# The first token block's second FFN product done plainly in two passes, with the other block's Strassen weight sums made in the second pass

## The chip, the cores and the metric

The kernel runs on one core of one Trainium2 chip. The metric is the time of one execution on the device, in microseconds (us); lower is better. PE is TensorE, DVE is VectorE, ACT is ScalarE, POOL is GpSimd, SP is SyncE, whose queue issues most of the DMAs here.

## The reference, cut to what matters

One layer of a streaming encoder: 16 meta tokens and 2048 tokens of width 1024 go through an S5 mixer with a gated linear unit, and then through a gated ConvFFN. The change lies in the ConvFFN alone, in its last product:

```python
def conv_ffn(xn, w_up, conv_w, conv_b, w_down):
    h = causal_dwconv(xn @ w_up, conv_w, conv_b)
    a, b = jnp.split(h, 2, axis=-1)
    return (jax.nn.silu(a) * b) @ w_down
```

Here `w_up` is 1024 x 5632, the convolution has 3 taps, and `w_down` is 2816 x 1024 (22 row blocks of 128). The result is added to the stream. The last 2048 rows are the output.

## The kernel before, in words

**Precision.** Each float32 operand is split into two float16 parts, high and low. A product is three matmuls (`mm3`, lines 75 to 78): high by high, high by low, low by high. All matmuls here are 128x128 by 128x512.

**Blocks.** The FFN runs twice, for kb = 0 and kb = 1, on 1024 tokens each. For each block `up` (line 1134 on) multiplies by `w_up` with 7 Strassen products per pair of column blocks, 22 pairs `m` in all, and `conv` does the convolution, the gate and the split of the activation into `act16[:, f, r, hi/lo, 512 tokens]`, where f is one of the 22 row blocks of `w_down` (NF = 22, NH = 11) and r is the half of the tokens. Then `down(kb)` multiplies by `w_down`.

**Strassen in `down`.** Both matrices are seen as 2 x 2: the activation by token half r and by f below or above 11, the weight by row half and by column half (512 columns). Seven products replace eight, in four stages with 2, 2, 2 and 1 products (`STAGES`). Each product takes 11 steps j, and each step is 4 token tiles (t4) of 3 matmuls, so `down` has 7 x 11 x 12 = 924 matmuls. The operands of a product are sums: the activation sums are made by `mix` (lines 1206 to 1220: POOL, DVE, ACT, DVE), 44 of them per block, with two scratch tiles that lie in the free part of `hc`; `add11` in `conv` (line 1119, POOL) makes one more sum for the rows above 11.

**Weights.** Every weight tile `wc` (128 x 2 x 512 float16, high and low) is a "unit". The units of both blocks stand in one list in the order of their use, and each takes the next of NR = 9 slots in turn. `w_unit` makes a unit for kb = 0: it has rows of `w_down` in one of NW = 4 staging tiles `fst` (float32, 512 KB, loaded by `w_load` on SP's queue); for 5 of 7 products POOL adds or subtracts two parts of it in place (lines 874 and 879); ACT writes the high part (line 880). `w_flush` then writes the low part on DVE (line 886), stores the unit to the DRAM buffer `wcd` from SP (line 887), and issues the next staging load if this unit was the last that uses its tile (lines 829 to 834). For kb = 1 a unit is only reloaded from `wcd` (line 859). `w_units(n + LD)` runs 5 units ahead of the matmuls. A flush happens only at the next call.

**Other traffic in `down(0)`.** `turn_hd` (line 1336) transposes the second block's inputs from DRAM into `hc` by DMA, 7 pairs, six of them in stage 0 at every second step. `load_res` brings the residual stream to tiles `res`, DVE adds the product to it (line 1323), and ACT's queue stores it to the output.

**Order.** The order on each engine is the order in which the program is written out; nothing reorders it. `later(d, fn)` puts a piece of work d ticks on, and `tick` is called once per `up` product and per `down` product step.

Of the kernel before, what the change touches and what calls it, by code (L numbers as in the profile page):

```python
# [15 lines left out]
P = 128  # L16
# [28 lines left out]
def tile_kernel(ctx: ExitStack, tc: tile.TileContext, x, meta, norm_mix, norm_ffn, w_in, lam_re, lam_im, log_dt,  # L45
# [20 lines left out]
    wcd = dram.tile([231, P, 2, 512], F16, name="wcd")  # L66
# [730 lines left out]
    kept = {u[:1] + u[2:]: i for i, u in enumerate(u for u in units if u[1] == 0)}  # L797
    for u in units:
        if u[1]:
            continue  # L800
        if u[0] == "u":
            need = [u[:3] + (0,)] + [u[:3] + (1,)] * (u[3] not in (1, 2))
        else:
            need = [u[:4] + (0,)] + [u[:3] + (u[3] // 2 * 2, 1)] * (u[2] == 2)
        for l in need:
            users[l] = u
            if l not in loads:
                loads.append(l)
    wst, wc, wtmp, ring, w_los, tdone = {}, {}, {}, {}, [], set()
# [6 lines left out]
    def w_load():  # L816
        if pos["load"] < len(loads):
            l = loads[pos["load"]]
            t = wst[l] = fw.tile([P, D], F32, tag="wst", bufs=NW, name=f"fst{pos['load']}")
            if l[0] == "u":  # L820
                m, ab = divmod(l[2], 2)
                c = 2 * m + NF * ab + l[3]
                SY.dma_start(out=t.rearrange("p (dk n) -> p dk n", n=P),
                             in_=w_up[0].rearrange("(dk p) n -> p dk n", p=P)[:, :, c * P:(c + 1) * P])
            else:
                s, j, i = l[2:]
                wd = w_down[0].rearrange("(a j p) (b n) -> j p a b n", a=2, p=P, n=512)[j]
                if s == 3:
                    SY.dma_start(out=t, in_=w_down[0, j * P:(j + 1) * P])
                elif i == 0:  # L830
                    SY.dma_start(out=t.rearrange("p (a n) -> p a n", a=2), in_=wd[:, :, int(s == 0)])
                else:
                    k = min(2, NH - j)
                    SY.dma_start(out=t.rearrange("p (a n) -> p a n", a=2)[:, 0:k],
                                 in_=w_down[0].rearrange("(f p) n -> p f n", p=P)[:, NH + j:NH + j + k, 512:1024])
            pos["load"] += 1
# [13 lines left out]
    def w_unit():  # L850
# [7 lines left out]
        if units[n][1]:  # L858
            SY.dma_start(out=w, in_=wcd[kept[units[n][:1] + units[n][2:]]])
            return  # L860
        if units[n][0] == "u":
# [5 lines left out]
            src = wtmp.pop((x_, m)) if i == 5 else st[src[0]][:, src[1]]  # L867
        else:
            k, kb, s, j, i = units[n]
            t = wst[k, kb, s, j, 0]  # L870

            if s == 2:
                src = t[:, hi_ if i == 0 else lo_]
                PO.tensor_tensor(src, src, wst[k, kb, s, j // 2 * 2, 1][:, hi_ if j % 2 else lo_], op=ALU.add)
            elif i == 1:
                src = t[:, hi_ if s == 0 else lo_]
            else:
                src, oth = (t[:, lo_], t[:, hi_]) if s in (0, 3) else (t[:, hi_], t[:, lo_])
                PO.tensor_tensor(src, src, oth, op=ALU.add if s == 3 else ALU.subtract)
# [3 lines left out]
    def w_flush():  # L883
        while w_los:
            w, src, u = w_los.pop(0)
            V.scalar_tensor_tensor(w[:, 1], src, GS, w[:, 0], op0=ALU.mult, op1=ALU.subtract)  # L886
            SY.dma_start(out=wcd[kept[u[:1] + u[2:]]], in_=w)
            for l in [l for l in wst if users[l] == u]:
                del wst[l]
                w_load()  # L890
# [198 lines left out]
    def conv(kb, m, e):  # L1089
# [12 lines left out]
        def taps():  # L1102
            V.scalar_tensor_tensor(y, hu[:, 1:17], cwt[:, 1, c:c + 1], y, op0=ALU.mult, op1=ALU.add)  # L1103
            V.scalar_tensor_tensor(y, hu[:, 0:16], cwt[:, 0, c:c + 1], y, op0=ALU.mult, op1=ALU.add)
            if ab and f < NH:
                for r, dst in ((0, yr[:, 0]), (1, actr[:, f, 1])):
                    V.scalar_tensor_tensor(dst, actr[:, f, r], AS, yr[:, r], op0=ALU.mult, op1=ALU.mult)
            elif ab:
                V.scalar_tensor_tensor(y, act[:, f], AS, y, op0=ALU.mult, op1=ALU.mult)

# [11 lines left out]
        if ab == 0:  # L1122
            later(6, lambda: A.activation(y, y, AF.Silu))
        elif f < NH:
# [104 lines left out]
    CTAG = {"12": (fl, "hu1"), "21": (fl, "hu1"), "11": (fl, "hu0"), "22": (fp, "yb")}  # L1229

    def down(kb):
# [8 lines left out]
        def load_res(c, q):  # L1240
            tt, cs_ = part(c, q)
            pool, tag = CTAG[c]
# [4 lines left out]
        def store_res(c, q, t):  # L1247
            tt, cs_ = part(c, q)
            for e in range(2):
                A.dma_start(out=o4[e, rows, tt, cs_][:, t], in_=res[c, q][64 * e:64 * e + 64, t])  # L1250

# [28 lines left out]
        if kb == 0:  # L1280
            for i, b in enumerate((0, 4, 8, 20, 12, 16)):
                put(0, 2 * i, turn_hd, b, b + 4)
            put(3, 1, turn_hd, 24, 28)

        for s, prods in enumerate(STAGES):
# [32 lines left out]
            for t4, i in banks:  # L1318
                for j in range(NH - 2, NH):
                    down_mm(j, t4, i)  # L1320
                for c, sign in prods[i][1:]:
                    h = res[c, t4 // 2][:, t4 % 2]
                    V.scalar_tensor_tensor(h, po[t4, i], sign / (GS * AS), h, op0=ALU.mult, op1=ALU.add)  # L1323
# [49 lines left out]
```

## Time and profile before

| what | value |
|---|---|
| runs | 2129.42, 2134.12, 2137.76 us; median 2134.12 us |
| the profiled execution | 2128.21 us; its span 2126.4 us, 1.8 us less |
| mean granted PE clock | 0.962 |
| `up(0)` | 770.6 to 1205.4 us |
| `down(0)` | 1205.4 to 1519.6 us |
| `up(1)` | 1519.6 to 1918.6 us |
| `down(1)` | 1918.6 to 2126.4 us |

The four stretches are cut where the first matmul of each begins. A matmul's own duration in the profile (380 ns) is longer than its share of PE's time, because matmuls overlap in the pipeline; the pace is read by counting matmuls in a window in which PE never stops. "Idle before" is time in which an engine did nothing before instructions of a group, with the instruction that released it. A DMA share of 1.00 means that all 16 DMA engines were busy all the time.

### The profile page before, as it was taken

What the parts mean: (1) busy time and instruction counts of PE and PEld (TensorE: products, weight loads), DVE (VectorE), ACT (ScalarE), POOL (GpSimd) and SP (SyncE); (2) the same over time, 40 slices, a digit from 0 to 9 for tenths busy, and PEclk for the clock granted to TensorE, in tenths of its full rate; (3) what the DMA queues carried; (4) which work ended last, traced back from release to release, by engine and by line L of the source; (5) the groups of instructions that cost most, each with busy time, mean ns of one, the idle gap of its engine ahead of it and who ended that gap; (6) DMA issues with size and microseconds to landing.
All of it is one profiled execution on the core that took longest, in us unless ns stands there. A gap on an engine that the chain in (4) does not pass through costs nothing. (4 is left out here: it accounts for less than half of the span.)

```text
span 2126.4 us, 29078 instructions
## 1 busy us (share of the span) xinstructions
PE 1925.9 (91%) x10860; PEld 954.7 (45%) x10860; DVE 1518.7 (71%) x2084; ACT 644.8 (30%) x1083; POOL 689.3 (32%) x727
## 2 busy tenths in 40 slices
PE   4688999699999999999999867676999999999999
PEld 3456556455444444444444323232444444444444
DVE  4489988944443459999999987954466666668882
ACT  4432322312222234444344422212122223232110
POOL 5221211410000025554666774734100001116740
PEclk9998999799999999999999989888999999999999
DMA  9956666957665565444434659554733333336443
GB/s 203 196 116 132 146 127 150 224 155 171 132 157 134 137 166 181 158 147 152 149 127 151 170 156 267 156 168 150 232 104 101 103 100 104 101 103 159 133 121 98
DMA packets 333449, 315.50 MB, mean 148 GB/s; under 512 B 149740, under 2 KB 237372, under 8 KB 333308
## 3 DMA queue, kind: packets, MB, share of 16 engines
q1 hardware_dynamic: 315388, 271.59, 49.4%
q0 software_dynamic: 8496, 27.30, 4.7%
q10 hardware_dynamic: 9424, 14.76, 2.6%
q8 instruction: 85, 1.39, 0.3%
q14 instruction: 56, 0.46, 0.1%
HBM read 175.17 MB, written 102.69 MB: 131 GB/s over the span
## 5 line engine op out<-in xcount | busy, mean ns | idle before, releaser
L78 PE MATMUL p<-hc,wc 128*128 128x512 f16 x1232 | 468.8, 381 | 6.5 <-DVE wc L886 6.5
L76 PE MATMUL p<-hc,wc 128*128 128x512 f16 x1232 | 468.8, 381 | 1.9 <-DMA hc<-hl 1.9
L77 PE MATMUL p<-hc,wc 128*128 128x512 f16 x1232 | 468.6, 380 | 0.9 <-DMA hc<-hl 0.9
L137 PE MATMUL g<-wg,yT 128*128 128x512 f16 x1536 | 334.2, 380 | 0.8 <-DMA yT<-yh 0.8
L77 PE MATMUL po<-wc,act 128*128 128x512 f16 x616 | 244.7, 397 | 80.4 <-DVE wc L886 80.4
L76 PE MATMUL po<-wc,act 128*128 128x512 f16 x616 | 243.5, 395 | 8.5 <-DVE res L1323 3.7
L78 PE MATMUL po<-wc,act 128*128 128x512 f16 x616 | 244.4, 397 | 0.0
L137 PEld LDWEIGHTS <-yT 128*128 128x128 f16 x1536 | 150.5, 98 | 182.9 <-issue 2.6
L886 DVE SCALAR_TENSOR_TENSOR wc<-fst,wc 128x512 f16<-128x512 f32 x209 | 199.0, 966 | 44.4 <-ACT wc L880 34.5
L880 ACT ACTIVATE wc<-fst 128x512 f16<-128x512 f32 x209 | 125.6, 625 | 245.0 <-POOL fst L847 120.3
L78 PEld LDWEIGHTS <-wc 128*128 128x128 f16 x1232 | 120.8, 98 | 154.7 <-DVE wc L886 8.8
L77 PEld LDWEIGHTS <-wc 128*128 128x128 f16 x1232 | 120.7, 98 | 139.9 <-issue 1.9
L76 PEld LDWEIGHTS <-wc 128*128 128x128 f16 x1232 | 120.6, 98 | 140.1 <-issue 3.5
L76 PE MATMUL u<-hnT,win 128*128 128x512 f16 (+2 forms) x352 | 113.1, 331 | 26.9 <-DMA hnT<-hl 17.0
L78 PEld LDWEIGHTS <-act 128*128 128x128 f16 x616 | 62.3, 101 | 163.5 <-issue 98.4
L1218 DVE TENSOR_TENSOR hc<-hc,hc 128x512 f32<-128x512 f32 x66 | 86.5, 1323 | 68.7 <-POOL hc L1216 42.7
L1219 ACT CAST act<-hc 128x512 f16<-128x512 f32 x88 | 54.2, 618 | 244.9 <-DVE hc L1218 148.0
L77 PE MATMUL u<-hnT,win 128*128 128x512 f16 (+2 forms) x352 | 112.9, 331 | 9.9 <-DMA hnT<-hl 9.9
L78 PE MATMUL u<-hnT,win 128*128 128x512 f16 (+2 forms) x352 | 112.7, 330 | 0.0
L1095 ACT ACTIVATE act<-hu,cwt 128x1024 f32<-128x1024 f32 x44 | 54.6, 1241 | 178.5 <-DVE hu L1187 129.8
L1095 ACT ACTIVATE y<-hu,cwt 128x1024 f32<-128x1024 f32 x44 | 54.6, 1241 | 162.3 <-DVE hu L1187 122.8
L1216 POOL TENSOR_TENSOR hc<-act 128x512 f32<-128x512 f16 x66 | 90.5, 1378 | 37.7 <-DVE hc L1218 37.7
(366 smaller groups left out, 3024.7 us busy)
## 6 DMA issues: line engine op xcount, KB each, us to landing
wcd<-wc SPq DMA_DIRECT2D x231, 256.0 KB, 2.3
wc<-wcd SPq DMA_DIRECT2D x231, 256.0 KB, 2.6
fst<-in_ffn_w_down_dram SPq DMA_DIRECT2D x49, 512.0 KB, 4.7
fst<-in_ffn_w_up_dram SPq DMA_DIRECT2D x44, 512.0 KB, 5.0
ud<-us SPq DMA_DIRECT2D x32, 258.0 KB, 4.8
U<-ud SPq DMA_DIRECT2D x16, 516.0 KB, 6.9
Toep<-kd SPq DMA_DIRECT2D x64, 128.0 KB, 5.5
yd<-yf POOLq DMA_DIRECT2D x8, 1024.0 KB, 6.5
```

What stands on the lines that cost most here:

```text
L76: PE.matmul(out=ps, lhsT=sh, rhs=mh, start=first, stop=False)
L77: PE.matmul(out=ps, lhsT=sh, rhs=ml, start=False, stop=False)
L78: PE.matmul(out=ps, lhsT=sl, rhs=mh, start=False, stop=last)
L137: PE.matmul(out=gps[t][o], lhsT=yT[t][:, a, dk], rhs=wg[b][:, dk, 512 * o:512 * o + 512], start=(dk == 0 and a + b == 0), stop=(dk == DK - ...
L880: A.activation(w[:, 0], src, AF.Copy, scale=GS)
L886: V.scalar_tensor_tensor(w[:, 1], src, GS, w[:, 0], op0=ALU.mult, op1=ALU.subtract)
L1095: A.activation(y, hu[:, 2:18], AF.Identity, bias=cwt[:, 3, c:c + 1], scale=cwt[:, 2, c:c + 1])
L1216: PO.tensor_tensor(t_, act16[:, fa_, ra, 1], act16[:, fb, rb, 1], op=op)
L1218: V.tensor_tensor(s_, s_, t_, op=ALU.add)
L1219: A.copy(act16[:, fd, rd, 0], s_)
```

## The change

For kb = 0 `down` no longer uses Strassen. It makes two passes, r = 0 and r = 1, over all 22 row blocks f; each step has both column halves n = 1, 0 and four token tiles, so a step is 24 matmuls, a pass 528, and both 1056. Eight PSUM banks hold a pass.

The units of kb = 0 are now: in pass 0 the 44 plain tiles ("p", row block f, column half n), made from a staging tile without any sum; in pass 1 the same 44 tiles, reloaded from `wcd`, and between them the 55 sums ("x", five for each j of 11) that kb = 1 needs, made by POOL, ACT and DVE and stored to `wcd`, but used by no matmul of kb = 0. The two Strassen tiles of kb = 1 that are no sums are plain tiles (`key`). Pass 1 loads all 22 row blocks of `w_down` into staging again, two for each j. Two of the five sums of a j are written to no staging half and share one buffer (`wtmp`). So `wcd` has 253 entries, and the first block's `mix` and `add11` are gone; `hi_all` and `lo_all` split a whole row block at once, for f below 11 too, where only half of it was split before. The seven pairs of transposes stand in pass 0 at f = 2, 4, .. 14, the residual loads of each pass at f = 6 and 8. In the last two steps of pass 1 the lead of the units is 2 instead of 5. `up`, and `down(1)` with its 924 matmuls and 77 reloads, stay as they were.

```diff
     for kb_ in range(2):
...
-        units += [("d", kb_, s, j, i) for s, n in ((0, 2), (1, 2), (2, 2), (3, 1)) for j in range(NH) for i in range(n)]
+        if kb_ == 0:
+            sums = [("x", 0, s, j, i) for j in range(NH) for s, i in ((1, 0), (2, 0), (0, 0), (2, 1), (3, 0))]
+            for r in range(2):
+                for f in range(NF):
+                    units += [("p", 0, r, f, 1), ("p", 0, r, f, 0)]
+                    units += sums[len(sums) * f // NF:len(sums) * (f + 1) // NF] if r else []
+        else:
+            units += [("d", 1, s, j, i) for s, n in ((0, 2), (1, 2), (2, 2), (3, 1)) for j in range(NH) for i in range(n)]
+    def key(u):
+        if u[0] == "u":
+            return ("u",) + u[2:]
+        if u[0] == "p":
+            return ("p",) + u[3:]
+        s, j, i = u[2:]
+        return {(1, 1): ("p", j, 0), (0, 1): ("p", j + NH, 1)}.get((s, i), ("x", s, j, i))
...
     def w_unit():
...
-        if units[n][1]:
-            SY.dma_start(out=w, in_=wcd[kept[units[n][:1] + units[n][2:]]])
+        if key(units[n]) in made:
+            SY.dma_start(out=w, in_=wcd[kept[key(units[n])]])
             return
+        made.add(key(units[n]))
...
+        elif units[n][0] == "p":
+            src = wst["p", units[n][3]][:, hi_ if units[n][4] else lo_]
         else:
...
+            if (s, i) in ((1, 0), (0, 0)):
+                src = fw.tile([P, 512], F32, tag="wtmp", bufs=1, name=f"xtmp{s}_{j}")
             else:
+                src = {(2, 0): b21, (2, 1): b22, (3, 0): b12}[s, i]
...
+            PO.tensor_tensor(src, one, oth, op=op)
         A.activation(w[:, 0], src, AF.Copy, scale=GS)
         w_los.append((w, src, units[n]))
...
     def conv(kb, m, e):
...
-            if ab and f < NH:
+            if ab and f < NH and kb:
...
+        elif kb == 0:
+            later(6, hi_all)
+            later(8, lo_all)
...
     def down(kb):
...
+        if kb == 0:
+            for r in range(2):
...
+                def step(f, ahead):
+                    w_units(uindex["p", 0, r, f, 0] + ahead)
+                    for _ in range(2):
+                        tick()
+                    if r == 0 and f in range(2, 16, 2):
+                        b = (0, 4, 8, 20, 12, 16, 24)[f // 2 - 1]
+                        turn_hd(b, b + 4)
+                    if f in (6, 8):
+                        for n in (1, 0):
+                            load_res(f"{r + 1}{n + 1}", f // 2 - 3)
...
+                for f0 in range(0, NF, 2):
+                    ends = f0 in (0, NF - 2)
+                    for f in (f0, f0 + 1):
+                        step(f, 2 if ends and f0 and r else LD)
+                        if not ends:
+                            for n, t4 in po:
+                                down_mm(f, n, t4)
+                    if ends:
+                        for n, t4 in po:
+                            for f in (f0, f0 + 1):
+                                down_mm(f, n, t4)
+                            if f0:
+                                c = f"{r + 1}{n + 1}"
+                                evict(c, t4, po[n, t4], 1)
...
+            return
```

Two places show how the change moves instructions. The first is SP's queue while the weight sums are made. Before, this is the third stage of `down(0)` (about 1400 to 1480 us): `fst` is a staging load, `wcd<-wc` the store of a finished unit.

```order
L831 DMA fst_12444<-in_ffn_w_down_dram 128x2x512
L831 DMA fst_12446<-in_ffn_w_down_dram 128x2x512
L887 DMA wcd<-wc_12385 128x1024
L887 DMA wcd<-wc_12450 128x1024
L834 DMA fst_12487<-in_ffn_w_down_dram 128x2x512
L887 DMA wcd<-wc_12453 128x1024
L887 DMA wcd<-wc_12491 128x1024
```

Now, in the middle of pass 1, on the same queue, for one j (two steps f); `wc<-wcd` is the reload of a plain tile for the next steps.

```order
L872 DMA wc_12473<-wcd 128x1024
L872 DMA wc_12475<-wcd 128x1024
L902 DMA wcd<-wc_12467 128x1024
L902 DMA wcd<-wc_12470 128x1024
L848 DMA fst_12505<-in_ffn_w_down_dram 128x1024
L848 DMA fst_12507<-in_ffn_w_down_dram 128x1024
L872 DMA wc_12516<-wcd 128x1024
L872 DMA wc_12518<-wcd 128x1024
L902 DMA wcd<-wc_12509 128x1024
L902 DMA wcd<-wc_12513 128x1024
L902 DMA wcd<-wc_12520 128x1024
```

The reloads that PE waits for now stand between the stores and loads of the sums, and one j takes 5 stores, 2 loads and 4 reloads where a step j of the old stage took 2 stores and 1.5 loads.

The second place is DVE at the start of `down(0)`. Before: the convolution's last multiplication (L1109) and, around the low parts of the weights (L886), the sums of `mix` (L1214) with their low parts (L1220).

```order
L1109 SCALAR_TENSOR_TENSOR y_21_1_11306<-act,y_21_1_11306 128x1024
L1214 TENSOR_TENSOR hc_4417<-hc_4417,act 128x512 x2
L886 SCALAR_TENSOR_TENSOR wc_11338<-fst_11146,wc_11338 128x512
L886 SCALAR_TENSOR_TENSOR wc_11340<-fst_11201,wc_11340 128x512
L1220 TENSOR_TENSOR act<-hc_4417,act 128x512 x2
L1115 TENSOR_TENSOR act<-y_21_0_11238,act 128x512 x2
L1214 TENSOR_TENSOR hc_4417<-hc_4417,act 128x512 x2
L886 SCALAR_TENSOR_TENSOR wc_11411<-fst_11201,wc_11411 128x512
```

Now, at the same place of DVE's order (L1124 is that multiplication, L901 the low part of a weight, L1130 `lo_all`):

```order
L1124 SCALAR_TENSOR_TENSOR y_21_1_11256<-act,y_21_1_11256 128x1024
L901 SCALAR_TENSOR_TENSOR wc_11279<-fst_11099,wc_11279 128x512
L901 SCALAR_TENSOR_TENSOR wc_11281<-fst_11153,wc_11281 128x512
L1130 TENSOR_TENSOR act<-y_21_0_11189,act 128x2x512
L901 SCALAR_TENSOR_TENSOR wc_11341<-fst_11153,wc_11341 128x512
L901 SCALAR_TENSOR_TENSOR wc_11343<-fst_11196,wc_11343 128x512
```

Between the low parts of the weights only the split of the last activations is left; after it DVE has nothing but low parts until the pass ends.

More of the change, by code (lines that the diff above doesn't have):

```diff
@@ L65, in tile_kernel @@
     hd = [dram.tile([8, 64, 28 * P], F16, name=f"hd{i}") for i in range(2)]
-    wcd = dram.tile([231, P, 2, 512], F16, name="wcd")
+    wcd = dram.tile([253, P, 2, 512], F16, name="wcd")
     def rstd_of(pool, ss, n, nm):
@@ L808, in tile_kernel @@
                 loads.append(l)
+    made = set()
     wst, wc, wtmp, ring, w_los, tdone = {}, {}, {}, {}, [], set()
@@ L886, in w_flush @@
             V.scalar_tensor_tensor(w[:, 1], src, GS, w[:, 0], op0=ALU.mult, op1=ALU.subtract)
-            SY.dma_start(out=wcd[kept[u[:1] + u[2:]]], in_=w)
+            SY.dma_start(out=wcd[kept[key(u)]], in_=w)
             for l in [l for l in wst if users[l] == u]:
@@ L1250, in store_res, with evict, down_mm @@
                 A.dma_start(out=o4[e, rows, tt, cs_][:, t], in_=res[c, q][64 * e:64 * e + 64, t])
+        def evict(c, t4, po_, sign):
+            h = res[c, t4 // 2][:, t4 % 2]
+            V.scalar_tensor_tensor(h, po_, sign / (GS * AS), h, op0=ALU.mult, op1=ALU.add)
+        if kb == 0:
+            for r in range(2):
+                po = {}
+                for n in (1, 0):
+                    for t4 in range(4):
+                        po[n, t4] = psum.tile([P, 512], F32, tag="uutt"[t4] if n else "vvyy"[t4], name=f"pq{r}_{n}_{t4}")
+                def step(f, ahead):
[6 more added lines that the diff above has]
+                    if f in (6, 8):
+                        for n in (1, 0):
+                            load_res(f"{r + 1}{n + 1}", f // 2 - 3)
+                def down_mm(f, n, t4):
+                    w = wc["p", 0, r, f, n]
+                    cs_ = slice(P * t4, P * t4 + P)
+                    mm3(po[n, t4], act16[:, f, r, 0, cs_], act16[:, f, r, 1, cs_], w[:, 0], w[:, 1], f == 0, f == NF - 1)
+                for f0 in range(0, NF, 2):
[12 more added lines that the diff above has]
+                                evict(c, t4, po[n, t4], 1)
+                                if t4 == 1:
+                                    w_flush()
+                                if r:
+                                    store_res(c, t4 // 2, t4 % 2)
+                                else:
+                                    later(2, lambda c=c, t4=t4: store_res(c, t4 // 2, t4 % 2))
+            return
         def mix_a(j):
@@ L1321, in down @@
                 for c, sign in prods[i][1:]:
-                    h = res[c, t4 // 2][:, t4 % 2]
-                    V.scalar_tensor_tensor(h, po[t4, i], sign / (GS * AS), h, op0=ALU.mult, op1=ALU.add)
+                    evict(c, t4, po[t4, i], sign)
                 if i == n - 1:
```

48 lines of the change are left out of this document (20 added, 28 removed).

## The prediction, made before the run

> **What bounds the kernel now.** I began with the busy time of each engine in the four stretches of the FFN (columns: stretch, length, then busy time and count of PE, weight loads, DVE, ACT, POOL, then granted clock, DMA share, GB/s).
>
> ```profile
> 770.60:1205.40 434.80, 422.71 (x2554) 199.21 (x2553) 407.86 (x459) 199.66 (x361) 252.59 (x259) 0.99 0.47 151
> 1205.40:1519.60 314.20, 231.03 (x925) 96.70 (x926) 221.11 (x240) 74.21 (x127) 169.61 (x127) 0.88 0.66 189
> 1519.60:1918.60 399.00, 399.00 (x1850) 180.87 (x1849) 249.24 (x299) 112.36 (x159) 35.68 (x59) 1.00 0.38 108
> 1918.60:2126.40 207.80, 199.55 (x924) 90.20 (x922) 150.15 (x163) 30.54 (x50) 91.50 (x64) 0.99 0.46 128
> ```
>
> The second and the fourth row do the same 924 matmuls, in 314.2 and 207.8 us. The fourth reloads its weights and the second makes them. In between PE works without a pause. So the first block's down product is the one stretch where PE is badly fed. What a matmul costs there undisturbed shows in a window of the fourth stretch in which PE never stops:
>
> ```profile
> 1990.00:2040.00 50.00, 50.00 (x233) 22.67 (x232) 45.41 (x45) 8.55 (x14) 35.39 (x24) 1.00 0.44 128
> ```
>
> 50.00 / 233 = 0.2146 us each. Next, what the matmuls on tile po waited for between 1200 and 1600 us, with the number of times behind:
>
> ```profile
> L77 PE MATMUL po<-wc,act x308: 376/379/634, 1205.6 to 1519.1; 128*128 128x512 f16 x154
>   DVE wc L886: 80.4, 25
>   DVE hu L1185: 2.3, 1
>   DVE hu L1193: 1.0, 1
> ```
>
> With two waits under 2 us, idle time is 85.5 us. 924 x 0.2146 is 198.3. That leaves 314.2 - 198.3 - 85.5 = 30.4 us of slow clock (a matmul shows 634 ns at worst, 379 normally), or 0.36 us for each us of idle time. All but 5 us of the idle time waits for the low part of a weight tile. Why that is late differs by stage:
>
> ```profile
> 1205.40:1330.00 124.60, 90.05 (x370) 37.98 (x371) 100.61 (x103) 35.63 (x62) 79.85 (x58) 0.89 0.80 214
> 1400.00:1480.00 80.00, 49.65 (x177) 19.73 (x176) 37.24 (x46) 15.16 (x26) 30.32 (x25) 0.82 0.41 128
> 1480.00:1519.60 39.60, 37.80 (x170) 16.74 (x169) 17.87 (x26) 5.56 (x9) 12.03 (x13) 0.97 0.92 272
> ```
>
> At first DVE is full (100.6 of 124.6 us) and the DMAs nearly so (0.80). From 1400 to 1480 nothing is full: it is a chain of latencies. The groups of instructions from 1205 to 1500 us, and SP's queue, show its links:
>
> ```profile
> L886 DVE SCALAR_TENSOR_TENSOR wc<-fst,wc 128x512 f16<-128x512 f32 x71 | 68.4, 997 | 8.1 <-ACT wc L880 6.7 <-ACT t8b L1164 1.2
> L1218 DVE TENSOR_TENSOR hc<-hc,hc 128x512 f32<-128x512 f32 x33 | 49.5, 1510 | 60.5 <-POOL hc L1216 42.7 <-POOL hc L1217 17.1
> L1216 POOL TENSOR_TENSOR hc<-act 128x512 f32<-128x512 f16 x33 | 44.0, 1342 | 0.0
> L879 POOL TENSOR_TENSOR fst<-fst 128x512 f32<-128x512 f32 x29 | 42.5, 1466 | 42.0 <-DMA fst<-in_ffn_w_down_dram 40.7 <-DVE wc L886 0.7 <-DVE res L1323 0.6
> L880 ACT ACTIVATE wc<-fst 128x512 f16<-128x512 f32 x69 | 41.4, 624 | 96.9 <-POOL fst L874 47.5 <-POOL fst L879 38.5 <-PE po L78 5.6
> ```
>
> ```profile
> 1419.57 0.69 SPq L834 DMA_DIRECT2D fst<-in_ffn_w_down_dram  x1
> 1420.35 8.94 SPq L887 DMA_DIRECT2D wcd<-wc  x2
> 1429.34 0.97 SPq L831 DMA_DIRECT2D fst<-in_ffn_w_down_dram  x2
> ```
>
> POOL waits for the load, ACT for POOL, DVE for ACT; SP's stores wait 8.9 us, and the next load stands behind them. A step there takes 9.8 us (1419.57 to 1429.34) where its 24 matmuls need 24 x 0.2146 = 5.15 us.
>
> **The change, part by part. Matmuls.** 8 products instead of 7: 1056 x 0.2146 = 226.6 us, 28.3 more, all on PE's path. They can't be hidden; they are the price. Against it stand 115.9 us of idle time and slow clock, so the question is how much of that stays.
>
> **DVE and POOL in the block.** The first block's 44 sums go (L1216, L1218 and their like), and with them what filled DVE at first. Pass 0 asks DVE for 2 low parts a step, 2 x 1.0 = 2.0 of 5.15 us, and POOL for nothing. Pass 1 asks per j (two steps, 10.3 us) for five of each: 5 x 1.47 = 7.3 us of POOL, 5.0 of DVE, 3.1 of ACT. Nothing is full. The queued convolution of the last pair stays, and with it the first waits, 2.3 + 1.0 = 3.3 us.
>
> **PE's chain in pass 0** is load, ACT, DVE, without POOL's sum; the loads run about 3 steps (15 us) ahead of their use. What can lack is throughput: SP must issue 7 pairs of transposes, one every two steps.
>
> ```profile
> 1272.78 7.86 SPq L1336 DMA_TRANSPOSE hc<-hd  x2
> 1285.13 0.54 SPq L887 DMA_DIRECT2D wcd<-wc  x1
> 1285.76 0.39 SPq L831 DMA_DIRECT2D fst<-in_ffn_w_down_dram  x1
> 1291.12 8.70 SPq L1336 DMA_TRANSPOSE hc<-hd  x2
> ```
>
> 8.3 + 4 stores x 0.54 + 2 loads x 0.39 = 11.2 us of SP for 10.3 us of PE. Over seven pairs that is 6 us late, and the residual loads add some; the lead of 15 us hides that if the DMAs keep up. The DMAs move 2.1 MB and 1.05 MB of transposes in these 10.3 us, 306 GB/s. At 214 / 0.80 = 267 GB/s, the rate of the first stage at full share, it takes them 11.8. I take 6 us of waiting, between 0 and 18: seven times 1.5 us, and 7.9 for 2.1 MB of residual.
>
> **PE's chain in pass 1** holds no sum: it needs only reloads, and the sums run beside it. But the reloads stand on SP behind the stores of the sums. The trace has the landing times (the DMA view from 1205.4 to 1519.6 us):
>
> ```profile
> fst<-in_ffn_w_down_dram SPq DMA_DIRECT2D x45, 512.0 KB, 4.8
> out_dram<-res ACTq DMA_DIRECT2D x26, 128.0 KB, 4.2
> wc<-wcd SPq DMA_DIRECT2D x7, 256.0 KB, 4.8
> ```
>
> A reload's slot was last used two steps before, half a step earlier than that step's end, so it can leave 1.5 steps = 7.7 us before its use: 2.9 us spare. Bytes: 55 stores and 44 reloads of 0.262 MB, 22 loads of 0.524, residual and output 4.2, in all 41.7 MB in 113.3 us, 368 GB/s. Three microseconds with full queues show what is possible:
>
> ```profile
> 1485.00:1486.00 1.00, 1.00 (x6) 0.49 (x5) 0.24 (x1) 0.63 (x1) 0.93 (x2) 1.00 1.05 426
> 1486.00:1487.00 1.00, 1.00 (x7) 0.41 (x5) 1.00 (x2) 0.56 (x1) 0.41 (x1) 1.00 1.02 404
> ```
>
> At 415 GB/s pass 1 takes 100 us of transfers, hidden; at the 272 / 0.92 = 296 of the last stage, 141, 28 us longer than PE. I take 8 us, nearer the first row, since pass 1 has no transposes.
>
> **The two seams.** At the start of pass 1 two steps are interleaved by bank, so the third step's second reload leaves only when the first two are over, and the fourth's stand behind it, two stores and two loads: about 10.3 + 2.5 + 4.8 us after the start for a tile wanted at 15.4: 2 us, and 5 with 16 output stores in the way. At the end the lead is cut to 2, so the next `up` has its first reloads issued only after the last stores: about 5 us (one landing, 4.8), where before they were issued ahead.
>
> **up(0).** Its last 105 us, and behind them, from 1100 us to the end, the group of low parts made from tile wtmp:
>
> ```profile
> L78 PE MATMUL p<-hc,wc 128*128 128x512 f16 x137 | 53.2, 388 | 6.5 <-DVE wc L886 6.5
> L1119 POOL TENSOR_TENSOR y<-y,act 128x512 f32<-128x512 f32 x10 | 15.3, 1527 | 0.4
> L1115 DVE TENSOR_TENSOR act<-y,act 128x512 f16<-128x512 f32 x12 | 8.3, 695 | 2.4 <-ACT act L1112 2.4
> L886 DVE SCALAR_TENSOR_TENSOR wc<-wtmp,wc 128x512 f16<-128x512 f32 x5 | 3.4, 680 | 0.0
> ```
>
> The sums L1119 go, and DVE is slower beside a busy POOL (the same low part takes 0.68 us here and 0.997 on average in the block). But rows f below 11 now split both halves, 0.7 us of DVE (L1115) more for each of 11, and DVE is 94% busy in this stretch (407.86 of 434.80). I take 4 us of gain, ends 9 (all idle time there with its clock) and -8 (11 x 0.7).
>
> **Sum.** Idle: 3.3 + 6 + 8 + 5 + 5 = 27.3; slow clock 0.36 x 27.3 = 9.8. The block takes 226.6 + 37.1 = 263.7 instead of 314.2, -50.5; with up(0) -54.5. The later stretches stay. On the profiled execution (2128.2) that is 2073.7; the median of the runs is 5.9 higher, so 2134.1 - 54.5 = 2079.6, say 2079.
>
> **A rule weighed.** After an idle time of 2.33 us the clock was low:
>
> ```profile
> 1205.39 0.38 PE L76 MATMUL po<-wc,act 128*128 128x512 f16 x1 [2.33 <-DVE hu L1185]
> 1206.14 0.63 PE L76 MATMUL po<-wc,act 128*128 128x512 f16 x1
> ```
>
> The Trainium skill, TensorE: Matmul & The Clock Gate (Part 1: The HAM clock gate), says that the clock is halved after an idle window of about 3.4 us. By it my short waits would cost no clock, and the sum would be 10 us less. The trace doesn't agree: 2.33 us were enough here.
>
> **Rivals.** (a) *All covered.* The queues keep up, PE never waits but at the start: 226.6 + 3.3 x 1.36 = 231, and 4 from up(0): 2134 - 83 - 4 = 2047. For it: 404 to 426 GB/s at peak, 15 us of lead in pass 0. Against: both seams. Chance 0.15.
>
> (b) *The DMAs become the bound.* The block now moves 76 MB (44 loads, 99 stores, 44 reloads, 14 transposes, 8.4 MB of residual and output). At the 267 GB/s of the transpose stage that is 285 us: 2134 - 29 = 2105. For it: 0.80 of share there with less demand. Against: transposes are in pass 0 only. Chance 0.17.
>
> (c) *Slower: one chain through SP.* The loads for j + 2 leave after step 2j, and their sums' stores stand ahead of reloads that leave after step 2j + 3: three steps, 15.4 us less 1.5 of issue. Load 4.8, sum, high, low 1.47 + 0.62 + 1.0, then the same again for the sum that waits for the shared buffer: 11.0 us. So 2.9 us are spare. Once a load lands later than 7.7 us, the stores block the reloads, and in the end everything goes in a row: 4.8 + 4 x 1.47 + 2 x 1.62 + 4.8 = 18.7 us for each j. Pass 1 takes 11 x 18.7 = 206 us, pass 0 113.3 and 1.36 x (3.3 + 6) = 126, the seams 10, the block 342: 2134 + 28 - 4 = 2158. For it: the same queue did that from 1400 to 1480. Against: there PE waited for the sums themselves. Chance 0.07.
>
> (d) *No gain*: half of (c), the block near 314. Chance 0.06.
>
> **How the numbers follow.** The forecast has 0.55. About 0.5% (10.7 us) is what a measurement of this kernel can tell from no change. Faster is the forecast, (a) and (b): 0.87; same is (d), 0.06; slower is (c), 0.07. The range leaves out (c), (d) and the far ends of (a) and (b): 2046 to 2114.
>
> **What would show it.** Right: about 1056 matmuls on the down tiles in 255 to 275 us, granted clock over 0.94 there, under 40 us of idle time, the waits for the low part of a weight nearly gone, and up(1) still at 399 us. For (b): a DMA share near 1.0 in both passes, PE waiting for reloads. For (c): stores on SP that wait for DVE in pass 1, and steps of 9 us. My terms are wrong if pass 0, not pass 1, holds most of the idle time, or if up(0) gets longer.

## The result, and the profile after

The changed kernel takes 2055.55 us (median of 4 runs, 2050.04 to 2063.94); on the same chip the kernel before took 2135.94 (4 runs). The ratio is 0.963, 95% interval 0.9589 to 0.9672. The forecast was 2079 us: the direction held, and the time came out 23.5 us below it, nearer to the 2047 us of rival (a). The profiled execution took 2054.77 us, its span is 2053.0, and its mean granted clock is 0.976 (0.962 before).

The same four stretches as before the change, cut in the same way (length, busy time of PE, weight loads, DVE, ACT and POOL with counts, granted clock, DMA share, GB/s):

```profile
770.50:1194.10 423.60, 418.88 (x2554) 198.61 (x2553) 401.48 (x439) 203.25 (x352) 230.43 (x239) 1.00 0.48 156
1194.10:1441.60 247.50, 233.02 (x1056) 104.08 (x1057) 101.78 (x123) 62.78 (x102) 81.68 (x62) 0.98 0.97 296
1441.60:1842.30 400.70, 399.02 (x1849) 180.75 (x1848) 249.81 (x299) 112.87 (x160) 35.77 (x61) 1.00 0.39 109
1842.30:2053.00 210.70, 202.67 (x925) 91.05 (x923) 150.49 (x163) 30.53 (x50) 91.61 (x65) 0.98 0.47 126
```

Read against the rows of before: `down(0)` went from 314.2 to 247.5 us (-66.7) and `up(0)` from 434.8 to 423.6 (-11.2). The last two stretches became 1.7 and 2.9 us longer. The 1.7 is a wait of `up(1)` for a reload, which ends at 1446.05. The 2.9 is slow clock: `down(1)` has a gap of 3.4 us in both kernels, and the 14 matmuls behind it took 5.90 us in the changed kernel (1902.90 to 1908.80) where those of the kernel before ran at full clock, at which 14 take 3.00. The sum is -73.3, and the spans differ by 73.4. In the second row DVE fell from 221.1 to 101.8 us and POOL from 169.6 to 81.7, while the DMA share rose from 0.66 to 0.97. PE has 132 matmuls more and the stretch is shorter.

What the matmuls on the tiles of `down(0)` waited for, in us, with the number of times behind:

```profile
L77 PE MATMUL pq<-wc,act x352: 377/379/631, 1194.3 to 1441.2; 128*128 128x512 f16 x176
  DMA wc<-wcd: 10.4, 6
  DVE hu L1217: 4.0, 1
  DVE hu L1209: 1.4, 1
```

The 80.4 us of waiting for low parts are gone. Apart from the start, what is left waits for reloads, all in pass 1. The first pass runs from 1194.1 to 1313.1 us, the second to 1441.6. Here is the middle of the first and the whole of the second:

```profile
1210.00:1300.00 90.00, 90.00 (x419) 40.79 (x417) 23.24 (x35) 19.31 (x33) 0.00 (x0) 1.00 1.08 279
1313.10:1441.60 128.50, 118.00 (x531) 52.30 (x530) 57.36 (x62) 32.40 (x52) 72.96 (x53) 0.97 0.92 307
```

In 90 us in which all seven pairs of transposes pass and the DMA share is at its ceiling, PE never stops: 419 x 0.2146 = 89.9. The last view is the DMA view of the block, 1194.1 to 1441 us (issues, KB each, median us to landing):

```profile
DMA packets 59538, 73.03 MB, mean 296 GB/s; under 512 B 32666, under 2 KB 32666, under 8 KB 59523
wcd<-wc SPq DMA_DIRECT2D x96, 256.0 KB, 5.1
wc<-wcd SPq DMA_DIRECT2D x45, 256.0 KB, 3.8
hc<-hd SPq DMA_TRANSPOSE x14, 8.3
```

### The profile page after: what moved, and what is told of

It reads as the page before. It is cut to its first block, busy times and chain, and to the rows that moved or that the text cites. A ratio compares the mean times of both kernels' runs of the same rounds, so it can differ in the third digit from the quotient of the medians.

```text
span 2053.0 us, 29208 instructions
## 1 busy us (share of the span) xinstructions
PE 1928.6 (94%) x10992; PEld 962.6 (47%) x10992; DVE 1393.9 (68%) x1948; ACT 637.6 (31%) x1050; POOL 580.3 (28%) x644
## 4 chain that ended last, share of the span: by engine, by line
PE 74%; DVE 9%; DMA 8%; SPq 3%; issue 2%; ACT 1%; POOL 1%; ACTq 0%; DVEq 0%; POOLq 0%
PE g L137 15%; PE p L76 12%; PE p L77 12%; PE p L78 12%; PE pq L76 2%; PE pq L77 2%; PE pq L78 2%; PE po L76 2%; PE po L77 2%; PE po L78 2%; DMA wc<-wcd 2%; DMA Z<-S 2%; DMA wcd<-wc 1%; DMA hnT<-hl 1%; PE yp L587 1%
## 5 line engine op out<-in xcount | busy, mean ns | idle before, releaser
L901 DVE SCALAR_TENSOR_TENSOR wc<-fst,wc 128x512 f16<-128x512 f32 x209 | 182.6, 882 | 110.2 <-ACT wc L895 94.3
L76 PE MATMUL pq<-wc,act 128*128 128x512 f16 x352 | 134.9, 383 | 15.9 <-DMA wc<-wcd 10.4
L77 PE MATMUL pq<-wc,act 128*128 128x512 f16 x352 | 134.9, 383 | 0.0
L78 PE MATMUL pq<-wc,act 128*128 128x512 f16 x352 | 134.8, 383 | 0.0
L76 PE MATMUL po<-wc,act 128*128 128x512 f16 x308 | 118.0, 383 | 3.4 <-DVE res L1279 3.4
L77 PE MATMUL po<-wc,act 128*128 128x512 f16 x308 | 117.9, 383 | 0.0
L78 PE MATMUL po<-wc,act 128*128 128x512 f16 x308 | 117.8, 382 | 0.0
```

Of the source, the lines that this page charges most:

```text
L76: PE.matmul(out=ps, lhsT=sh, rhs=mh, start=first, stop=False)
L77: PE.matmul(out=ps, lhsT=sh, rhs=ml, start=False, stop=False)
L78: PE.matmul(out=ps, lhsT=sl, rhs=mh, start=False, stop=last)
```

## The experiments

Three questions: whether the first block's activation sums were what stalled the old block, and by what mechanism; what made `up(0)` faster; and what the 10 us of reload waits in pass 1 hang on. Where one figure stands for a block, it is read from one profiled execution.

### Was it the activation sums?

**The kernel before without the first block's activation sums** (`nomix[0]` holds for the first block; `conv` splits both halves as in the changed kernel).

```diff
     def mix(op, dst, a, b, eng=PO):
+        if nomix[0]:
+            return
```

> The kernel before the change, Strassen and all its 924 matmuls, weight sums and transfers in down(0), but without the first block's activation sums (mix and add11 are left out and both halves are split as in the changed kernel, so the first block's result is not the reference's). Theory: two separate causes made the old down(0) slow, DVE full of those sums at first and a chain from load to POOL to ACT to DVE later. Then the first 125 us shrink to about 90 to 100, the steps of the third stage stay near 9.8 us, and down(0) takes 270 to 290 us instead of 314. Rival 1, the activation sums were all of it: 205 to 235 us. Rival 2, only the weight chain mattered: over 300 us.

Measured: 2022.9 us (a single execution; before on that chip 2133.73). The block and its waits:

```profile
1198.80:1412.50 213.70, 203.38 (x924) 91.02 (x925) 104.90 (x134) 49.42 (x81) 77.22 (x62) 0.98 0.94 278
  DVE res L1336: 8.5, 1
  DVE wc L886: 0.7, 2
```

100.5 us less, and the wait for low parts falls from 80.4 to 0.7 us, in all stages. The first rival came out, and the theory of two separate causes fell. Yet every weight sum is still made, in the same order, with the same loads and stores on SP. So the third stage (1400 to 1480 us before) was not slow by the chain from load to low part alone: that chain is still there and runs at PE's pace.

**The same, and the weight sums left out too** (the weights are then split unsummed).

```diff
-                PO.tensor_tensor(src, src, oth, op=ALU.add if s == 3 else ALU.subtract)
+                pass
```

> As the run without activation sums, and the weight sums on POOL are left out too (ACT reads the staging tile directly; the results of both blocks are not the reference's). Loads, stores and matmuls are the same. Theory: the chain is mostly the load and its place behind the stores on SP, so a step of the third stage falls from 9.8 to 7 to 8.5 us and down(0) takes 240 to 270 us. Rival, POOL's sums were the chain: the third stage runs at PE's pace, 5.15 us a step, and down(0) takes 205 to 230 us.

Measured: 2025.81 us (a single execution), the block 212.1 (1202.0 to 1414.1). Without activation sums beside them, the weight sums cost nothing that shows.

**The kernel before with its activation sums on DVE and ACT only.** As many operations there as before, none on POOL (`first[0]` holds for the first block). The sums are of the high halves alone: POOL's part is left out, not moved.

```diff
-        if op == ALU.add and ra:
+        if first[0]:
+            V.tensor_tensor(s_, act16[:, fa_, ra, 0], act16[:, fb, rb, 0], op=op)
+            if eng is V:
+                V.tensor_tensor(s_, s_, act16[:, fb, rb, 1], op=op)
+        elif op == ALU.add and ra:
```

> The kernel before, where the first block's activation sums are made with as many operations on DVE and ACT as before but none on POOL (they add high halves alone, so the numbers that are summed are not those of the reference; up makes both splits directly as in the changed kernel). Theory: what stalled the old block was the tie between engines: DVE in its queue waited for POOL, POOL stood behind weight sums that waited for loads; without POOL in it the old block takes 215 to 235 us, close to the 213.7 without any activation sums. Rival: DVE's and ACT's own work for the sums was too much beside the weight splits: the block stays above 270 us.

Measured: 2056.97 us, ratio 0.9669 (0.9632 to 0.9705). The block, then its waits:

```profile
1200.90:1445.00 244.10, 214.32 (x924) 93.34 (x925) 181.92 (x238) 73.51 (x125) 91.45 (x62) 0.93 0.85 243
```

```profile
  DVE wc L886: 18.9, 8
  DVE res L1338: 8.8, 1
```

244.1 us is a little above the range of the theory and far below the rival's 270. So of the 100 us that the sums cost the old block, 70 came from having POOL in them and 30 from DVE's and ACT's own work. One part of the 70 is order, and the old profile shows it. Here is one step of the third stage, on SP, POOL and DVE:

```profile
1409.78 0.97 SPq L831 DMA_DIRECT2D fst<-in_ffn_w_down_dram  x2
1410.86 8.62 SPq L887 DMA_DIRECT2D wcd<-wc  x2
```

```profile
1414.37 1.26 POOL L874 TENSOR_TENSOR fst<-fst,fst 128x512 f32<-128x512 f32 x1 [6.13 <-DMA fst<-in_ffn_w_down_dram]
1415.58 1.16 POOL L1216 TENSOR_TENSOR hc<-act 128x512 f32<-128x512 f16 x1
```

```profile
1416.77 1.73 DVE L1218 TENSOR_TENSOR hc<-hc,hc 128x512 f32<-128x512 f32 x1 [5.59 <-POOL hc L1216]
1418.43 1.28 DVE L886 SCALAR_TENSOR_TENSOR wc<-fst,wc 128x512 f16<-128x512 f32 x2
```

POOL's weight sum L874 waits for a load, its activation sum L1216 stands behind that, DVE stands idle 5.59 us for L1216 before L1218, and the low parts L886 stand behind L1218. By the order of the program the first of the two belongs to a unit whose high part ACT had written at 1409.96. Its store stands in SP's queue until the low part is made, and the next load, behind it, leaves at 1419.57. So a load left only after the load before it had landed and passed through POOL and DVE: from 1409.78 that makes 4.59 + 1.21 + 1.19 + 1.66 + 1.14 = 9.79 us, the whole step. Without activation sums nothing that stands ahead of that low part on DVE waits for the next load, and the loop is open.

The other part is DVE's pace beside a busy POOL. How the 70 us divide between the two over the whole block is not shown. L1218 took 1510 ns, and here DVE's groups for the sums, which are partly of other forms, run at these means (busy us, mean ns, then idle time before):

```profile
L1223 DVE TENSOR_TENSOR hc<-act 128x512 f32<-128x512 f16 x44 | 38.4, 890 | 0.0
L1234 DVE TENSOR_TENSOR act<-hc,act 128x512 f16<-128x512 f32 x44 | 34.0, 804 | 0.9 <-ACT act L1233 0.8
```

Of the forms that both have, the low part of a weight (L886) went from 997 to 826 ns and that of a sum (L1220, here L1234) from 723 to 804. DVE is still busy 181.9 us, but its sums no longer wait for another engine; that moved the time about as much as the whole rewrite did, though with incomplete sums.

### What made up(0) faster?

**The changed kernel with the first block's two POOL sums per row put back** (their result goes to a tile that nothing reads).

```diff
+            if f >= NH:
+                for i in range(2):
+                    later(6, lambda i=i: PO.tensor_tensor(hu[:, 2:10].rearrange("p a b -> p (a b)"), yr[:, 0],
+                                                               act16[:, f - NH, 0, i], op=ALU.add))
```

> The changed kernel with the two POOL additions per row block f of 11 and above put back into up(0), written to a dead tile, so that they cost POOL time and wait for the same inputs, but change nothing. up(0) took 434.8 us before the change and 423.6 after it. If those POOL additions slowed DVE and so PE (theory), up(0) goes back to 431 to 435 us and the whole gets 8 to 11 us slower. If the gain in up(0) came from the way the activations are split now, or from the different loads at its end (rival), up(0) stays within 2 us of 423.6.

Measured: 2070.32 us, ratio 0.9686 (0.963 to 0.9741). Its `up(0)`, and what PE waited for there:

```profile
782.30:1217.20 434.90, 419.92 (x2554) 198.07 (x2553) 413.30 (x439) 203.19 (x352) 259.09 (x257) 1.00 0.47 151
```

```profile
  DVE wc L901: 9.9, 7
```

434.9 us, as before the change (434.8): the whole 11.2 us is these POOL sums. (The time of the whole kernel is some 12 us longer by the ratios, whose intervals overlap.) Nothing reads them in this run. They slow DVE, which makes PE's weights; PE waited 9.9 us for those here and 0.5 in the changed kernel. The last stretch of `up(0)` before (1100 to 1205 us) and after (1100 to 1194), operations of one shape:

```profile
L886 DVE SCALAR_TENSOR_TENSOR wc<-fst,wc 128x512 f16<-128x512 f32 x31 | 33.0, 1065 | 2.7 <-ACT t8b L1164 2.5
L1109 DVE SCALAR_TENSOR_TENSOR y<-act,y 128x1024 f32<-128x1024 f32 x4 | 6.8, 1699 | 0.1
```

```profile
L901 DVE SCALAR_TENSOR_TENSOR wc<-fst,wc 128x512 f16<-128x512 f32 x31 | 27.5, 887 | 2.6 <-ACT wc L895 1.2 <-ACT t8b L1188 1.2
L1124 DVE SCALAR_TENSOR_TENSOR y<-act,y 128x1024 f32<-128x1024 f32 x4 | 4.9, 1225 | 0.1
```

The low parts alone are 5.5 us of DVE there, on an engine that is busy 94% of `up(0)`. In the same two answers an operation that reads one operand from PSUM did not change (`hu<-p,hu`):

```profile
L1191 DVE TENSOR_TENSOR hu<-p,hu 128x512 f32<-128x512 f32 x10 | 6.4, 677 | 0.0
```

```profile
L1215 DVE TENSOR_TENSOR hu<-p,hu 128x512 f32<-128x512 f32 x10 | 6.4, 677 | 0.0
```

The Trainium skill (SBUF — State Buffer, SBUF: two separate sides) has a rule for this: DVE and GpSimd share a pair of SBUF ports, which an operation of DVE with two SBUF inputs and one of GpSimd that reads SBUF take in turns, each for the whole instruction. The trace agrees in these rows: two forms with two SBUF inputs took 887 and 1225 ns and, beside POOL's sums, 1065 and 1699; the one with a PSUM input stayed at 677. In the same stretch of the run with the sums put back the two forms took 1053 and 1793. But other forms with two SBUF inputs took the same in both answers (`y<-hu,cwt,y` 1728 ns twice, `act<-hu,cwt,act` 1582 and 1580), so the form alone does not decide. What POOL does at that moment goes with it: before the change, L1109 took 1.23 us at 1131.79, beside POOL operations on 4 elements, and 2.17 us at 1139.66, beside a weight sum. So the activation sums can also act by shifting POOL's other work; how much is which is not shown.

### What bounds the new block?

**128 of the 1056 matmuls left out** (the third of three for f from 7 to 14).

```diff
+                    if f in range(7, 15):
...
+                        return
```

> The changed kernel with 128 matmuls fewer: in steps f = 7 to 14 of both passes the third of the three matmuls (low by high) is left out, so the result is less exact. All transfers stay. If PE bounds down(0) (theory), it takes 128 x 0.2146 = 27 us less, 247.5 to about 220, and the whole is 25 to 29 us faster. If the DMAs bound it (rival b: their share is 0.97 there), the time comes back as waits for reloads and weights, and the whole is 0 to 10 us faster.

Measured: 2043.88 us, ratio 0.9583 (0.9546 to 0.962). The block is 241.1 us (1198.8 to 1439.9), 6.4 less, where 128 x 0.2146 would be 27.5. Its waits grew:

```profile
  DMA wc<-wcd: 15.5, 8
  ACT wc L895: 5.1, 4
```

The whole is some 10 us faster by the ratios, whose intervals overlap, where the theory had 25 to 29. So PE is not the only bound. What feeds it has little to spare.

**Each pair of transposes issued twice**, 14 pairs instead of 7.

```diff
                         turn_hd(b, b + 4)
+                        turn_hd(b, b + 4)
```

> The changed kernel with each of the seven pairs of transposes in pass 0 issued twice (the same data to the same place), 7.3 MB and some 58 us of SP's queue more. Pass 0 takes 119 us now. If the DMAs and SP are full there already (their share is 1.01 to 1.16 from 1210 to 1300 us), pass 0 gets 30 to 50 us longer. If pass 0 still has much of its lead of 15 us and idle transfer time (my forecast priced 0 to 18 us of waiting, and none came), it gets less than 15 us longer.

Measured: 2084.41 us (a single execution), the block 282.4 (+35), with new waits for high parts in pass 0:

```profile
  ACT wc L895: 21.3, 5
  DMA wc<-wcd: 12.7, 9
```

Pass 0 hides seven pairs and has no room for seven more: rival (b) of the prediction was close in pass 0.

**The reloads of pass 1 issued from ACT's queue** instead of SP's.

```diff
-            SY.dma_start(out=w, in_=wcd[kept[key(units[n])]])
+            (A if units[n][0] == "p" else SY).dma_start(out=w, in_=wcd[kept[key(units[n])]])
```

> The changed kernel with pass 1's reloads of the plain tiles issued from ACT's queue instead of SP's, so that they no longer stand behind the stores and loads of the weight sums. Same bytes. If PE's waits for reloads in pass 1 (10.4 us, six times) come from their place on SP, they fall under 4 us and the whole gets 6 to 12 us faster. If they come from full DMAs, or from the output stores that would now stand on the same queue, the whole stays within 4 us.

Measured: 2050.07 us, ratio 0.9614 (0.9579 to 0.9648); the block 250.0, the reload waits 9.8 us in 5 against 10.4 in 6. Moving them did not free them. ACT's queue has holds of its own there, the 16 output stores among them, so this run does not tell a place in a queue from the transfers.

**The seams**: the stores of pass 0's results spread over nine steps, and the PSUM banks of the two column halves exchanged.

```diff
-psum.tile([P, 512], F32, tag="uutt"[t4] if n else "vvyy"[t4], name=f"pq{r}_{n}_{t4}")
+psum.tile([P, 512], F32, tag="yyvv"[t4] if n else "ttuu"[t4], name=f"pq{r}_{n}_{t4}")
...
-                                    later(2, lambda c=c, t4=t4: store_res(c, t4 // 2, t4 % 2))
+                                    later(4 + 2 * t4 + 8 * (1 - n), lambda c=c, t4=t4: store_res(c, t4 // 2, t4 % 2))
```

> The changed kernel with two seams mended. The 16 output stores of pass 0 leave one pair a step in pass 1 instead of all at its second step (PE waited 4.5 us for a reload there), and the first banks of a pass are those that up(0) has long left (PE waited 1.4 and 4.0 us for an eviction). If PE bounds the block apart from such waits, 9.9 us of idle time and some clock go: 8 to 14 us faster than the changed kernel. If the DMAs bound it, the waits come back elsewhere: 0 to 4 us faster.

Measured: 2056.9 us, ratio 0.9636 (0.9596 to 0.9676); the block 253.0, reload waits 12.9 us. The wait at the seam is 3.7 us instead of 4.5, and others grew: not the 8 to 14 us of the theory.

**The same with 11.5 MB less to move**: 22 plain tiles are made again in pass 1 from the staging tiles that the sums need anyway, instead of being stored and reloaded (rows taken in the order j, j + 11, the sums in another order).

```diff
+    def remade(u):
+        return u[0] == "p" and (u[3] < NH) == (u[4] == 1)
...
-        if key(units[n]) in made:
+        if key(units[n]) in made and not remade(units[n]):
...
-            SY.dma_start(out=wcd[kept[key(u)]], in_=w)
+            if not remade(u):
+                SY.dma_start(out=wcd[kept[key(u)]], in_=w)
```

> As e7, and with 11.5 MB less traffic in down(0): 22 of the 44 plain tiles are not stored in pass 0 and not reloaded in pass 1, but made again by ACT and DVE from the staging tiles that pass 1 loads anyway (its steps go j, j + 11). DVE makes 7 instead of 5 low parts for each j. If the DMAs bound the block (73 MB in 247.5 us now), it falls to 230 to 238 us, 10 to 18 us faster than the changed kernel, with a DMA share under 0.9. If PE and its seams bound it, no faster than e7. If DVE becomes late beside POOL, slower than e7.

Measured: 2057.09 us, ratio 0.9623 (0.9589 to 0.9657); the block 256.8. Pass 1 with its seam, and the waits:

```profile
1315.00:1450.50 135.50, 121.53 (x524) 52.90 (x523) 66.51 (x80) 41.03 (x69) 67.44 (x51) 0.94 0.79 251
```

```profile
  DMA wc<-wcd: 13.8, 6
```

At a share of 0.79 and with half the reloads the waits are no shorter. So bandwidth alone is not what holds PE in pass 1. The run also gives ACT and DVE more splits, and SP's stores stand 43.0 us for low parts.

**Pass 1 opened step by step** instead of two steps at once, bank by bank.

```diff
-                    ends = f0 in (0, NF - 2)
+                    ends = f0 in (r * (NF - 2), NF - 2)
```

> The second pass no longer opens bank by bank over two steps; its first two steps run like the middle ones, step by step. Theory: in the changed kernel the slots of the pass's first two loads come free only when both steps are done, some 10 us after the pass starts, so the first reload issued in it stands in SP's queue and PE waits 4.5 us near 1334; run plainly, the slots come free after 5.2 us and that wait goes: the block 243 us against 247.5, the kernel about 2051. Rival: the wait comes from the transfers of the seam (stores of results, the last kept splits) and stays, block 247 to 248. Second rival: the seam itself needs the opening by banks (the last sums of the first pass being moved out), and a wait of 2 to 4 us for DVE appears at the seam instead.

Measured: 2054.4 us, ratio 0.9676 (0.9633 to 0.972); the block 247.2, reload waits 10.1, the one at the seam 4.95. By itself the opening is not the cause either.

**The residual loads one at a time**, at steps 6, 8, 10 and 12.

```diff
-                    if f in (6, 8):
-                        for n in (1, 0):
-                            load_res(f"{r + 1}{n + 1}", f // 2 - 3)
+                    if f in (6, 8, 10, 12):
+                        load_res(f"{r + 1}{1 + f // 2 % 2}", int(f > 9))
```

> The residual loads of each pass, two tiles at step 6 and two at step 8, are issued one tile a step pair, at steps 6, 8, 10 and 12. Theory: the four loads at once hold SP's queue 2.5 to 3 us (and up to 9 in the runs with spread stores), and the reloads behind them come late: the waits for reloads after 1345, some 6 us of the 10.4, shrink to 2 or less and the block to about 243. Rival: the waits after 1345 belong to the free slots and to the length of the queue as such, and stay at 4 to 6 us, block 246 to 248.

Measured: 2054.04 us, ratio 0.9661 (0.9611 to 0.9711), in its profile:

```profile
1209.60:1453.00 243.40, 232.57 (x1056) 104.27 (x1057) 103.72 (x123) 62.79 (x102) 82.94 (x62) 0.98 0.97 301
```

```profile
  DMA wc<-wcd: 6.8, 4
```

The block is 4.1 us shorter. The waits behind the seam fall from 5.9 us to 1.9, as the theory had it: four loads in a row did hold the reloads. The time of the whole kernel cannot show 4 us (0.2%).

**Queues set free**: the spread residual loads, the spread stores, and the stores of the kept sums issued from ACT, so that no reload on SP stands behind an unfinished split.

```diff
-            SY.dma_start(out=wcd[kept[key(u)]], in_=w)
+            (A if u[0] == "x" else SY).dma_start(out=wcd[kept[key(u)]], in_=w)
```

> The residual loads one at a time as in the run before; the 16 stores of the first pass's results spread over nine steps instead of standing 11.6 us long in ACT's queue; and the stores of the kept splits of the sums issued on ACT, so that on SP no reload stands behind a split that isn't finished. Theory: what is left of the waits (6.8 us, 4.9 of it near the seam) is order in the queues: ACT's result stores hold the next high parts, SP waits for their splits, the reload stands behind. With the three taken apart the reload waits fall to 2 us or less and the block from 243.4 to 238 to 240. Rival: the reloads wait for their slots, or for the transfers (the DMA share is 0.97 there), not for a place in a queue: the waits stay at 5 us or more, and the block at 243 or above; more on ACT could also bring waits for its high parts.

Measured: 2059.18 us, ratio 0.9644 (0.9619 to 0.9669); the block 253.7, reload waits 14.1 us in 8. The theory fell. SP's queue at the seam of this run (start, length, line) shows what it did instead:

```profile
1311.90 18.17 SPq L872 DMA_DIRECT2D wc<-wcd  x5
1330.16 0.88 SPq L848 DMA_DIRECT2D fst<-in_ffn_w_down_dram  x2
```

Five reloads take 18 us to leave although no store stands between them: between 1300 and 1345 us SP's reloads stood 14.5 us for PE's last use of a slot. Over pass 1 of this run they also stood 30.3 us for stores to `wcd` to land, against 0.9 over the block of the changed kernel, so the stores on ACT held them in another way. At the seam of the changed kernel the same place looks like this, on SP (a row left out) and then on ACT:

```profile
1318.20 5.50 SPq L872 DMA_DIRECT2D wc<-wcd  x2
1325.84 0.92 SPq L902 DMA_DIRECT2D wcd<-wc  x2
...
1327.81 0.90 SPq L872 DMA_DIRECT2D wc<-wcd  x2
```

```profile
1313.08 0.63 ACT L895 ACTIVATE wc<-xtmp 128x512 f16<-128x512 f32 x1 [4.01 <-PE pq L78]
1313.16 11.20 ACTq L1275 DMA_DIRECT2D out_dram<-res  x16
1324.46 1.15 ACT L895 ACTIVATE wc<-fst 128x512 f16<-128x512 f32 x2 [10.75 <-DMA out_dram<-res]
```

Sixteen output stores hold ACT's queue for 11.2 us. The next high parts are made behind them, SP's stores wait for those until 1325.84, and the reload behind leaves at 1327.81; PE waits for it from 1329.4 to 1333.8. With the stores spread (the seams run) that hold is gone, and the opening by banks, which keeps the first slots until both steps are over, remains; with the plain opening alone the stores remain. Each was taken away alone, and they were not tried together. That either of them suffices for the wait is what I infer; it is not shown.

**What stays open.** Why pass 1 waits in every variant. The lead itself is not too short. Where nothing holds SP's queue, a reload leaves when PE has used its slot for the last time, two steps before; over the block SP's reloads stood 38.4 us for that, 26 times:

```profile
SPq L872 <- PE pq L78: 38.4, 26, 3.2
```

```profile
1391.28 2.91 SPq L872 DMA_DIRECT2D wc<-wcd  x2
```

The first reload of this pair leaves at 1391.28 and, counted off in order, its tile is wanted at 1398.86: a lead of 7.6 us, as the prediction had it (7.7). A reload lands in 4.6 us at the median of pass 1, so some 3 us are spare. Five of the six waits fall on reloads that left 2.6 to 9.0 us after their slot was free; the sixth (1431.91) is at the end, where the pass closes bank by bank. One such place is in the middle of the pass:

```profile
1352.35 3.09 SPq L1270 DMA_DIRECT2D res<-h1d  x4
1355.54 2.05 SPq L902 DMA_DIRECT2D wcd<-wc  x3
1358.19 1.43 SPq L872 DMA_DIRECT2D wc<-wcd  x2
```

The first of these two reloads left 3.7 us after its slot was free, and PE waited for it until 1364.09. What makes SP late at the seam in every variant stays open. A larger ring of slots was not tried.

## Why the prediction was right, point by point

**The price** held: 1056 matmuls at 0.2146 us, 90.00 / 419 = 0.2148 in pass 0.

**The old stall** was read wrongly, and this is the step that failed. The prediction gave it two causes, a full DVE at first and, "from 1400 to 1480 nothing is full: it is a chain of latencies", with the links load, POOL, ACT, DVE. The run without activation sums keeps those links and waits 0.7 us. The cause was one in all stages: the activation sums, and seven tenths of their cost was that POOL took part in them. The rows for it were quoted in the prediction (L1218 with 60.5 us idle for POOL). I passed over them: the sums are another job in the same queues, and that job closes the loop from one load to the next. That the forecast came out all the same is in part luck: the change removes these sums, whichever way the stall is read.

**The terms of the sum.** Forecast against measured idle time in us: start 3.3, measured 4.0 + 1.4; pass 0's transposes 6, measured 0; reloads in pass 1 8, measured 10.4 - 4.5 = 5.9; seam between the passes 5, measured 4.5; end seam 5, measured 1.7 (behind the cut, at 1446.05). Of the block's 247.5 us, 226.6 are matmuls and 14.4 idle time inside it (the 1.4 lies before its first matmul), which leaves 6.5 for slow clock and rest where the forecast had 9.8. So the block came out 16.2 us below the forecast's 263.7, about halfway to the 231 of rival (a). `up(0)` gained 11.2 where I took 4, outside my ends of 9 and -8: I had counted its idle time, and mis-sized what POOL's sums take from DVE. The later stretches gave back 4.6. On the profiled executions that is 18.8 us. The other 5 are chance: I added 5.9 us from the profiled execution to the median, and for the changed kernel that distance is 0.8.

**Pass 0.** I had taken SP's 11.2 us of issue for every 10.3 of PE as 6 us of waiting. SP took longer still: from the first pair (1210.21) to the seventh (1284.45) 12.4 us a pair. The lead of 15 us covered that. Doubled transposes showed where the cover ends.

**"PE's chain in pass 1 holds no sum"** was true of the data and not of the queues: at the seam the reload stood behind stores of sums, and these behind ACT's output stores.

**The clock.** Each matmul starts 0.21 us after the one before at full clock and 0.43 when it is halved. After the gap of 4.47 us in the changed kernel (start, duration, and the first with its wait; rows left out):

```profile
1333.83 0.58 PE L76 MATMUL pq<-wc,act 128*128 128x512 f16 x1 [4.47 <-DMA wc<-wcd]
...
1364.09 0.38 PE L76 MATMUL pq<-wc,act 128*128 128x512 f16 x1 [1.50 <-DMA wc<-wcd]
```

12 matmuls took 4.99 us there instead of 2.58 (1333.83 to 1338.82), so that gap cost 2.4 us more; after the start's gap of 3.98 us 7 took 2.83 instead of 1.50, 1.3 more. The gap of 1.50 us has only full-speed matmuls behind it, as had gaps of 1.64 us in the queues run and 1.77 in the plain opening. So slow clock comes in stretches behind long gaps, not as my 0.36 us per us of idle time, and not behind each of them: 2.08 us were enough in the run with fewer matmuls (1393.96), while 2.83 us in the kernel before (1361.11) and its 3.42 us in `down(1)` (1978.96) had none. The rule of the Trainium skill that was weighed (TensorE: Matmul & The Clock Gate, Part 1: The HAM clock gate) makes it a matter of idle windows, and in this it was nearer than my factor: waits of up to 1.77 us cost no clock in the cases above. Its length of about 3.4 us is longer than gaps that sufficed: 2.08 us in the run above, 2.33 before the change, and 2.52 in the seams run.

**The rivals.** (a) had the block at 231 and was too bright by the two seams and pass 1. (b) was half right: the share is 0.97, yet the DMAs deliver. (c) did not come: the highest wait is 4.5 us. Of my signs, the clock over 0.94 (0.98), under 40 us of idle time, and low parts no longer waited for came true; `up(1)` took 400.7 against 399. The 255 to 275 us for the block did not (247.5), and of the signs for (b) both showed in part: shares of 1.01 and 0.92 in the two passes, and waits for reloads.

## What to carry to other kernels

Where a wait names engine A, look in A's queue for what stands ahead, and ask of each such instruction whom it waits for: here the low parts of weights waited behind unrelated sums that waited for POOL, and POOL for a load that those low parts held back. Splitting an operation over DVE and POOL ties two in-order queues together; leaving POOL's part out of the sums gained about as much as making the product without sums. A prefetch that leaves 7.6 us ahead and lands in 4 to 6 has about 3 us for everything that stands before it in its queue: count that, entry by entry. Moving single entries took away some waits here and made others.

## What the runs showed of the hardware

- Two DVE operations with two SBUF inputs took 20 and 39% longer beside POOL's sums, and one with a PSUM input took the same time; the rows are under the question on `up(0)`.
- PE can run without a pause while the DMA share reads 1.08 for 90 us; a full share is no stall by itself.
- Sixteen DMA issues of 128 KB in a row held ACT's queue for 11.2 us, 0.70 us each, and the next ACT instruction stood behind them.
- After a gap of 3.4 us the clock was low for 14 matmuls in the changed kernel and not at all in the kernel before, at the same place of the program. It need not fall at once either: in the seams run a wait of 3.69 us ended at 1358.39, the first five matmuls ran at full clock, and the slow ones came from 1359.47 to 1362.80.
